# A two-layer hybrid decoder trunk on one core: block inverse on four row strips, score products in bursts of sixteen, low-rank products of both halves in one burst

## The chip, the cores and the metric

One core of a Trainium2 chip runs the whole program. The metric is the device time of one execution in microseconds (us); lower is better. Before the change the median of three runs is 2336.88 us (2336.01 to 2342.26).

## The reference

A residual stream x of 1024 tokens by 1024 channels passes through two layers. Each normalizes it, projects it once to a wide row, gives the parts of that row to three causal token mixers (pooling, retention, RWKV-7), gates and projects the three results, merges them, projects once more and adds. The part that matters here is RWKV-7: 8 heads of 64 channels, with a state that is updated token by token.

```python
def rwkv7_time_mix(p, shift_mu, w0, w2, a0, a2, k_k, k_a, r_k, ln_w, ln_b):
    ...
    w = -jax.nn.softplus(-(w0 + jnp.tanh(wl) @ w2)) - 0.5
    decay = jnp.exp(-jnp.exp(w.astype(jnp.float32)))
    a = jax.nn.sigmoid(a0 + al @ a2)
    ...
    def step(S, inp):
        r_t, w_t, k_t, v_t, a_t, b_t = inp
        sa = jnp.einsum('bhvk,bhk->bhv', S, a_t)
        S = (S * w_t[:, :, None, :] + sa[..., None] * b_t[:, :, None, :]
             + v_t[..., None] * k_t[:, :, None, :])
        return S, jnp.einsum('bhvk,bhk->bhv', S, r_t)
    _, y = lax.scan(step, jnp.zeros((B, H, N, N), jnp.float32), xs)
    ...

def hybrid_layer(x, c_act, positions, ...):
    mod = c_act @ w_ada + b_ada
    shift, scale, gate = jnp.split(mod[:, None, :], 3, axis=-1)
    h = rms_norm(x, norm_g) * (1.0 + scale) + shift
    proj = h @ w_in
    ...
    branches = jnp.stack([o_pool, o_ret, o_rwkv], axis=2)
    y = jnp.einsum('btnw,nwd->btnd', branches, w_branch)
    gates = jax.nn.sigmoid(gate_logits.reshape(B, T, N_BRANCHES, D))
    merged = jnp.sum(gates * y, axis=2)
    return x + gate * (merged @ w_out)
```

## The kernel before

**The wide products.** Channels lie on the 128 partitions, tokens on the free axis in two halves of 512. Each weight tile is split into a high and a low part (wh, wl), each activation too (hhi, hlo, later oG and olo, mhi and mlo), and three products of 128 rows by 128 columns by 512 tokens replace one in full precision. They go to three accumulators `acc` in PSUM. They are the bulk of TensorE's instructions and are called wide products here.

**The mixers.** They are generators ("tasks") in lanes. The loop over the projection's columns issues wide products; after each, `pump` lets every lane whose due time has come issue a step. A task yields a time after which it wants to go on. A pair of RWKV heads (`rwkv_task(l, hp, ...)`, four per layer, one after another in the lane "rwkv") does, for each half h of the sequence:

- the low-rank products (`lora_mm`): three products for the decay (tile lw) and three for the rate a (tile la), each with 64 rows, alternating between the two 64-row halves of the array; ACT takes them through a tanh into sg and aT;
- elementwise work on DVE, ACT and POOL, transposes (vt, bt);
- the score products (tile g): for groups of four chunks of 64 tokens, each with two heads on the two 64-row halves, eight products of 64 rows to two PSUM banks, after which DVE masks them into Z, GQ and KG.

Then for both halves together the inverse of a unit triangular 64 by 64 matrix for each of 16 chunks by 2 heads is formed. The two 32 by 32 diagonal blocks are inverted on DVE (tiles M and tm). The lower left block is the product of three blocks: m1 = (off-diagonal block) x (first inverse), then m2 = (second inverse) x m1. Each is 32 products of 32 by 32 by 32; all of m1 read partitions 0 to 31 (one strip of 32 rows of the array), all of m2 partitions 32 to 63. They are issued in two bursts of 16 for m1 and two for m2, each to one bank of the pool `mx`, each followed by one copy on ACT. At last a chain over the 16 chunks updates the state (tiles cy, ch, xst, S).

Products in plain fp32 (g, m, and all of 128 columns) are run by the chip as two passes, so the profile has two records for each; the products from split tiles have one.

**What sets the order.** The program first records all operations (`Prog.record`), each with the planner's clock at that point as its priority. `slots` gives the tiles their buffers, `needs` finds which operation must follow which, and `weave` is a list scheduler: with a cost for each operation (`cost`) it simulates the five engines and writes the instructions in the order in which they could start, those of lower priority value first among the ready ones. What it writes is what each engine's queue runs, in order. So a change of a cost or of a dependency shifts where the later products of all tasks stand among the wide ones. For a product of 32 rows the cost before was 32 ns for the load and 32 for the product (`o.load, o.occ`), and a change between products of 128, 64 and 32 rows cost nothing.

**PSUM.** Three banks acc, two `mx` (shared by the mixers), two `cy` and one `ch` (both used by rwkv_task alone, after the start).

Of the kernel before, what the change touches and what calls it, by code (L numbers as in the profile page):

```python
# [18 lines left out]
P = 128  # L19
# [188 lines left out]
class Op:  # L208
    __slots__ = ("eng", "what", "args", "kw", "outs", "ins", "prio", "lane", "pred", "succ", "n", "i",
                 "dur", "occ", "load", "twice", "lock", "est", "start", "end", "left", "table", "acc", "arr", "seq", "know", "waits", "part")  # L210
# [50 lines left out]
class Prog:  # L261


    def __init__(self):
        self.ops, self.bufs, self.width, self.pools = [], [], {}, {}
        self.now = lambda: 0.0
        self.lane = [None]
        for e in ENG:
            setattr(self, e, Engine(self, e))
# [41 lines left out]
    def needs(self):  # L311
# [6 lines left out]
        for chain in self.chains.values():  # L318
            old = []
            for b in chain:  # L320
# [21 lines left out]
                old = mine  # L342
        for o in self.ops:
# [3 lines left out]
    def cost(self, o):  # L347
# [6 lines left out]
        if o.eng == "PE":  # L354
# [3 lines left out]
            o.twice = rhs.dtype != F32R and w != "transpose"  # L358
            if rhs.dtype == F32R:
# [3 lines left out]
            else:  # L363
                o.load, o.occ, o.dur = (55, 53, 272) if k == 64 else (32, 32, 191)
# [41 lines left out]
    def weave(self):  # L406
# [13 lines left out]
        landed, table, pe = [0.0] * 8, 0, [0.0, 0.0]  # L420
# [11 lines left out]
        while len(order) < len(ops):  # L432
# [23 lines left out]
            if e == "PE":  # L456
# [3 lines left out]
                m = max(pe[1], max(pe[0], o.est) + ld)  # L460
                if o.twice:
# [19 lines left out]
            for i in o.succ:  # L481
# [4 lines left out]
                elif kind != "a" and e != "PE":  # L486
# [3 lines left out]
                if r == s:  # L490
# [62 lines left out]
def trunk_kernel(ctx, tc, xT, cvec, pos, vecs, consts, w_ada, w_all, pool_w, lora_w, out):  # L553
# [35 lines left out]
    t_cs = slot("cs", 3)  # L589
    mi = lambda s: t_mi(s)[:, 0:HF]  # L590
# [9 lines left out]
    def cyt(s):  # L600
        return ps_c.tile([P, HF], F32, tag="cy", name=nm(s))

# [603 lines left out]
    def rwkv_task(l, hp, kT, rT, vp, lt, lw):  # L1206
# [17 lines left out]
        bvs = []  # L1224
        for h in range(2):
            cr = slice(8 * h, 8 * h + 8)
            yield wait(*lt[h])
            pss = [mx("lw"), cyt("la")]
            lora_mm(pss, lw, hc, lt[h])
            sg = t_ri("sg")  # L1230
            nc.scalar.activation(sg, pss[0], AF.Tanh, bias=vv(l, "w0", hp), scale=0.5)
            yield 400
            aT = t_ri("aT")
            nc.scalar.activation(aT, pss[1], AF.Tanh, bias=vv(l, "a0", hp), scale=0.5)
# [60 lines left out]
            for q in range(2):  # L1295
# [5 lines left out]
                yield 1300  # L1301
            for q in range(2):
                c0 = 8 * h + 4 * q
                yield wait(AR)
                gps = [mx("g"), cyt("g")]
                for j in range(4):
                    for hd in range(2):
                        rows = slice(64 * hd, 64 * hd + 64)
                        mmul(gps[hd][:, j * P : (j + 1) * P], jt(BK, rows, c0 + j), jt(AR, rows, c0 + j))
                lo, hi = slice(0, 64), slice(64, 128)  # L1310
                for hd in range(2):
                    own, other = (lo, hi) if hd == 0 else (hi, lo)
                    g3 = gps[hd].rearrange("p (u n) -> p u n", n=P)
# [824 lines left out]
```

## Time and profile before

| | us |
|---|---|
| timed runs, median (lowest to highest) | 2336.88 (2336.01 to 2342.26) |
| the profiled execution, its own time | 2333.52 |
| its span, first to last instruction | 2331.7 |
| TensorE busy | 2287.5 (98%) |
| VectorE (DVE) busy | 1442.1 (62%) |
| ScalarE (ACT) busy | 855.8 (37%) |
| GpSimd (POOL) busy | 817.4 (35%) |

The mean clock granted to TensorE over the span is 0.996. A row of the timeline has the start, the time to the last end, engine, line, operation, the tile written and those read, rows and columns of the weights, shape, and the number of instructions that were merged into the row. PE is TensorE's products, PEld its weight loads. Nearly all rows carry one line number, since all operations are issued by the planner's loop; they are told apart by their tiles. The profile leaves out numbers in names, so m1 and m2 both stand as m; m<-G,Z is m1 and m<-Z,G is m2.

### The profile page before, as it was taken

The page shows a single profiled execution, that of the slowest core. Times are in us where ns is not written, and L with a number is a line of the kernel's source. Part 1 is how long each engine was busy: PE and PEld are TensorE (multiplying, and loading weights), DVE is VectorE, ACT ScalarE, POOL GpSimd, SP SyncE. Part 2 cuts the span into 40 slices and gives each one's busy share as a digit, 9 for nine tenths or more (in the row PEclk, how much of TensorE's full clock was granted, in tenths as well). Part 3 has the DMA queues.
Part 4 walks back from the last instruction along what each step waited for, and adds up shares of the span by engine and source line. Part 5 has one row for each costly group of instructions (what it writes and reads, how often), then busy time and mean ns, then how long its engine had stood idle before and what let it go on. Part 6 is the DMA issues. An engine that isn't in the chain of part 4 may idle for free. (4 is left out here: it accounts for less than half of the span.)

```text
span 2331.7 us, 33818 instructions
## 1 busy us (share of the span) xinstructions
PE 2287.5 (98%) x12520; PEld 1907.6 (82%) x12520; DVE 1442.1 (62%) x2826; ACT 855.8 (37%) x1706; POOL 817.4 (35%) x714
## 2 busy tenths in 40 slices
PE   5999999999999999999999999999999999999998
PEld 4888888888888888888887888888788888888888
DVE  8776578468568744669546746855864884413544
ACT  5633442433433333223444334234433423311343
POOL 5222233234142333463442233323323333326441
PEclk9999999999999999999999999999999999999999
DMA  8132112112213325767422211211211131545442
GB/s 283 39 110 78 42 46 92 42 41 70 73 55 99 102 61 178 237 194 250 139 82 64 69 41 44 94 34 49 78 61 42 56 118 52 162 126 163 118 145 82
DMA packets 126517, 227.79 MB, mean 98 GB/s; under 512 B 14352, under 2 KB 17680, under 8 KB 126352
## 3 DMA queue, kind: packets, MB, share of 16 engines
q1 hardware_dynamic: 126352, 225.63, 30.9%
q8 instruction: 98, 1.61, 0.3%
q14 instruction: 67, 0.55, 0.1%
HBM read 176.56 MB, written 49.02 MB: 97 GB/s over the span
## 5 line engine op out<-in xcount | busy, mean ns | idle before, releaser
L549 PE MATMUL acc<-hhi,wh 128*128 128x512 f32 x2000 | 806.7, 403 | 0.0
L549 PE MATMUL acc<-hhi,wl 128*128 128x512 f32 x2000 | 806.6, 403 | 0.0
L549 POOL TENSOR_TENSOR wl<-wr,wh 128x512 fp32r<-128x512 f32 x342 | 458.5, 1341 | 991.4 <-ACT wh L549 947.3
L549 PE MATMUL acc<-hlo,wh 128*128 128x512 f32 x2000 | 805.1, 403 | 0.0
L549 ACT CAST wh<-wr 128x512 fp32r<-128x512 f32 x342 | 212.2, 620 | 655.2 <-PE acc L549 441.7
L549 PEld LDWEIGHTS acc<-hlo,wh 128*128 128x128 f32 x2000 | 378.0, 189 | 66.6 <-issue 2.2
L549 PEld LDWEIGHTS acc<-hhi,wl 128*128 128x128 f32 x2000 | 378.1, 189 | 66.5 <-issue 2.2
L549 PEld LDWEIGHTS acc<-hhi,wh 128*128 128x128 f32 x2000 | 378.2, 189 | 65.6 <-issue 1.1
L549 PE MATMUL acc<-oG,wl 128*128 128x512 f32 x384 | 149.9, 390 | 0.0
L549 PE MATMUL acc<-oG,wh 128*128 128x512 f32 x384 | 149.7, 390 | 0.0
L549 PE MATMUL acc<-olo,wh 128*128 128x512 f32 x384 | 149.7, 390 | 0.0
L549 DVE SCALAR_TENSOR_TENSOR S<-ch,pc,SP 64x64 f32<-64x64 f32 x224 | 63.3, 282 | 91.3 <-PE ch L549 85.2
L549 ACT COPY xst<-Z 64x64 f32<-64x64 f32 x256 | 62.4, 244 | 152.7 <-DVE Z L549 149.5
L549 DVE COPY xst<-cy 64x64 f32<-64x64 f32 x256 | 55.4, 216 | 90.7 <-PE cy L549 65.2
L549 DVE TENSOR_TENSOR tm<-VB 64x30 f32<-64x30 f32 (+14 forms) x240 | 105.4, 439 | 7.4
L549 DVE TENSOR_TENSOR VB<-VB,tm 64x30 f32<-64x30 f32 (+14 forms) x240 | 99.4, 414 | 7.5
L549 DVE COPY Z<-ch 64x128 f32<-64x128 f32 x128 | 36.0, 282 | 93.1 <-PE ch L549 92.5
L549 ACT ACTIVATE gsg<-acc 128x512 f32<-128x512 f32 x88 | 52.4, 596 | 91.9 <-PE acc L549 79.6
L549 PEld LDWEIGHTS acc<-olo,wh 128*128 128x128 f32 x384 | 72.1, 188 | 15.0
L549 PEld LDWEIGHTS acc<-oG,wh 128*128 128x128 f32 x384 | 72.1, 188 | 15.0 <-DVE gs L549 0.2
L549 PEld LDWEIGHTS acc<-oG,wl 128*128 128x128 f32 x384 | 72.1, 188 | 15.0
L549 DVE SCALAR_TENSOR_TENSOR gs<-gs,acc 128x512 f32<-128x512 f32 x64 | 43.7, 684 | 46.1 <-PE acc L549 45.0
(270 smaller groups left out, 3693.6 us busy)
## 6 DMA issues: line engine op xcount, KB each, us to landing
wr<-in_w_all SPq DMA_DIRECT2D x364, 256.0 KB, 2.7
gd<-gsg SPq DMA_DIRECT2D x88, 256.0 KB, 2.0
gs<-gd SPq DMA_DIRECT2D x88, 256.0 KB, 2.8
wada<-in_w_ada SPq DMA_DIRECT2D x70, 256.0 KB, 3.3
ol<-od SPq DMA_DIRECT2D x64, 256.0 KB, 3.2
ringG<-in_w_ada SPq DMA_DIRECT2D x26, 256.0 KB, 5.1
x<-in_xT SPq DMA_DIRECT2D x16, 256.0 KB, 5.0
od<-po SPq DMA_DIRECT2D x16, 256.0 KB, 2.2
```

The costliest lines, as they stand in the source:

```text
L549: f(*[put(x) for x in o.args], **{k: put(x) for k, x in o.kw.items()})
```

## The change

Four things are edited.

- **m1 and m2.** The 32 products of each are dealt to four strips (`quad`): strip g works on partitions 32g to 32g+31, on head g // 2 and on eight of the 16 chunks, and writes to a PSUM bank of its own (mx, cy, ch, cy) on the same partitions. Consecutive products go to strips 0, 1, 2, 3. To bring the operands to the strips, two tiles W1 and W2 (`t_mq`, names mn and mt) are filled by copies on ACT and DVE. Each of m1 and m2 is one burst of 32 products.
- **Score products.** Both groups of four chunks of a half are issued as one burst of 16 products to four banks; the masking on DVE follows for both.
- **Low-rank products.** Both halves h are issued at the head of the task as one burst of 12 products to four banks, and the tanh of both halves follow.
- **The planner.** A new list `bursts` makes every product of a burst wait for everything that any of them waits for (kind "x"), so that none starts before all can. The cost of a product of 32 rows becomes 15 and 15 ns, and a change between 128, 64 and 32 rows costs 110 or 200 ns.

```diff
@@ Prog.needs
+        for a, b in self.bursts:
+            own = [o for o in self.ops[a:b] if o.eng == "PE"]
+            union = {q for o in own for q in o.pred if not a <= q < b}
+            for o in own:
+                for q in union:
+                    o.pred.setdefault(q, "x")
@@ Prog.cost
-                o.load, o.occ, o.dur = (55, 53, 272) if k == 64 else (32, 32, 191)
+                o.load, o.occ, o.dur = (55, 53, 272) if k == 64 else (15, 15, 191)
@@ Prog.weave
+                if o.rows != rows:
+                    m, rows = m + (110 if o.rows == 32 else 200), o.rows
@@ rwkv_task
+        yield wait(*lt[0], *lt[1])
+        pss = [[mx("lw"), cyt("la")], [cht("lw"), cyt("la")]]
+        at = len(nc.ops)
+        for h in range(2):
+            lora_mm(pss[h], lw, hc, lt[h])
+        nc.bursts.append((at, len(nc.ops)))
...
-            for q in range(2):
-                c0 = 8 * h + 4 * q
-                yield wait(AR)
-                gps = [mx("g"), cyt("g")]
+            yield wait(AR)
+            gps = [[mx("g"), cyt("g")], [cht("g"), cyt("g")]]
+            at = len(nc.ops)
+            for q in range(2):
                 for j in range(4):
                     for hd in range(2):
-                        rows = slice(64 * hd, 64 * hd + 64)
-                        mmul(gps[hd][:, j * P : (j + 1) * P], jt(BK, rows, c0 + j), jt(AR, rows, c0 + j))
+                        rows, c = slice(64 * hd, 64 * hd + 64), 8 * h + 4 * q + j
+                        mmul(gps[q][hd][:, j * P : (j + 1) * P], jt(BK, rows, c), jt(AR, rows, c))
+            nc.bursts.append((at, len(nc.ops)))
...
+        W1, W2 = t_mq("mn"), t_mq("mt")
+        quad = [(slice(32 * g, 32 * g + 32), g // 2, slice(8 * (g % 2), 8 * (g % 2) + 8)) for g in range(4)]
+        for rows, hd, c8 in quad[1:]:
+            nc.scalar.copy(q4(W1, rows), Z[0:32, c8, 64 * hd + 32 : 64 * hd + 64])
...
-        for q in range(2):
-            ps = mx("m1")
-            for u in range(16):
-                uu = 16 * q + u
-                mmul(ps[32:64, u * 32 : u * 32 + 32], N_[0:32, uu, 32:64], t1(slice(0, 32), uu))
...
+        def quads(name, lhsT, rhs):
+            pss = [mx(name), cyt(name), cht(name), cyt(name)]
+            at = len(nc.ops)
+            for v in range(8):
+                for g, (rows, hd, c8) in enumerate(quad):
+                    u, o = 2 * (c8.start + v) + hd, slice(32 * v, 32 * v + 32)
+                    mmul(pss[g][rows, o], lhsT(g, rows, u, o), rhs(g, rows, u, o))
+            nc.bursts.append((at, len(nc.ops)))
+            return pss
...
+        for g, (rows, hd, c8) in enumerate(quad):
+            (nc.scalar.copy, nc.vector.tensor_copy)[g % 2](W2[rows, 0:256], pss[g][rows, 0:256])
```

TensorE's order at the block inverse of the first pair of heads, before: the two bursts of m1 (m_325 and m_326), three wide products between them, five more, and then m2.

```order
L549 MATMUL m_325_1814<-G_1077,Z_918 32x32 x16
L549 MATMUL acc_1761<-hhi_606,wh_1717 128x512
L549 MATMUL acc_1761<-hlo_618,wh_1717 128x512
L549 MATMUL acc_1761<-hhi_606,wl_1723 128x512
L549 MATMUL m_326_1838<-G_1077,Z_918 32x32 x16
L549 MATMUL acc_1761<-hhi_627,wh_1717 128x512
L549 MATMUL acc_1761<-hlo_641,wh_1717 128x512
L549 MATMUL acc_1761<-hhi_627,wl_1723 128x512
L549 MATMUL acc_1789<-hhi_540,wh_1717 128x512
L549 MATMUL acc_1789<-hlo_556,wh_1717 128x512
L549 MATMUL m_327_1864<-Z_918,G_1077 32x32 x16
```

The same place after: the head of the one burst of m1, whose four banks m_327 to m_330 belong to the four strips (this round of four stands there eight times).

```order
L561 MATMUL acc_1785<-hhi_565,wh_1715 128x512
L561 MATMUL m_327_1838<-G_1116,Z_940 32x32
L561 MATMUL m_328_1840<-mn_1202 32x32
L561 MATMUL m_329_1842<-mn_1202 32x32
L561 MATMUL m_330_1844<-mn_1202 32x32
```

And what stands between its last product and the one burst of m2:

```order
L561 MATMUL m_330_1844<-mn_1202 32x32
L561 MATMUL acc_1785<-hlo_582,wh_1715 128x512
L561 MATMUL acc_1785<-hhi_565,wl_1723 128x512
L561 MATMUL acc_1785<-hhi_616,wh_1715 128x512
L561 MATMUL acc_1785<-hlo_630,wh_1715 128x512
L561 MATMUL acc_1785<-hhi_616,wl_1723 128x512
L561 MATMUL acc_1785<-hhi_638,wh_1715 128x512
L561 MATMUL acc_1785<-hlo_650,wh_1715 128x512
L561 MATMUL m_331_1890<-mt_1835 32x32
```

Four bursts have become two, with seven wide products between them; for the eight blocks of both layers it is seven in six of them, six in one and four in one. Over the program the before has 18 bursts of 16 products and 7 of 32, the after 16 of 32.

TensorE's score products, before, where a burst broke (third pair of heads, first layer): the four products of one half of the array, a wide product, the four of the other half. Elsewhere the two banks alternate in a burst of eight.

```order
L549 MATMUL acc_4524<-hhi_373,wh_4409 128x512
L549 MATMUL g_4572<-AR_4281,BK_4460 128x128 x4
L549 MATMUL acc_4524<-hlo_388,wh_4409 128x512
L549 MATMUL g_4582<-AR_4281,BK_4460 128x128 x4
L549 MATMUL rvt_4588<-cst,rv_4393 128x128 x4
```

After (first pair of heads, the middle of a burst): the second group of four chunks follows the first at once, here from banks g_1080 and g_1083 to g_1094 and g_1096.

```order
L561 MATMUL g_1080<-AR_701,BK_902 128x128
L561 MATMUL g_1083<-AR_701,BK_902 128x128
L561 MATMUL g_1094<-AR_701,BK_902 128x128
L561 MATMUL g_1096<-AR_701,BK_902 128x128
L561 MATMUL g_1094<-AR_701,BK_902 128x128
```

The before has 30 bursts of 8 and 4 of 4; the after 16 of 16, none broken.

TensorE's low-rank products at the first pair of heads, before: one half's six products, and wide ones behind them (the other half's follow 200 rows later).

```order
L549 MATMUL lw_788<-lt_733,lw_527 128x512
L549 MATMUL la_791<-lt_733,lw_527 128x512
L549 MATMUL lw_788<-lt_740,lw_527 128x512
L549 MATMUL la_791<-lt_740,lw_527 128x512
L549 MATMUL lw_788<-lt_733,lw_538 128x512
L549 MATMUL la_791<-lt_733,lw_538 128x512
L549 MATMUL acc_786<-hlo_347,wh_448 128x512
```

After: the other half's six (lw_799, la_801) stand right behind.

```order
L561 MATMUL lw_788<-lt_733,lw_538 128x512
L561 MATMUL la_792<-lt_733,lw_538 128x512
L561 MATMUL lw_799<-lt_737,lw_527 128x512
L561 MATMUL la_801<-lt_737,lw_527 128x512
L561 MATMUL lw_799<-lt_746,lw_527 128x512
L561 MATMUL la_801<-lt_746,lw_527 128x512
L561 MATMUL lw_799<-lt_737,lw_538 128x512
L561 MATMUL la_801<-lt_737,lw_538 128x512
L561 MATMUL acc_786<-hlo_347,wh_448 128x512
```

The before has 17 such bursts (15 of 6, one broken in two), the after 8 of 12. On ACT the order grows from 1697 to 1761 instructions, on DVE from 2826 to 2866; POOL has as many as before, and SP issues four DMAs fewer (86 gate tiles are stored early and fetched again instead of 88).

More of the change, by code (lines that the diff above doesn't have):

```diff
@@ L209 @@
     __slots__ = ("eng", "what", "args", "kw", "outs", "ins", "prio", "lane", "pred", "succ", "n", "i",
-                 "dur", "occ", "load", "twice", "lock", "est", "start", "end", "left", "table", "acc", "arr", "seq", "know", "waits", "part")
+                 "dur", "occ", "load", "twice", "lock", "est", "start", "end", "left", "table", "acc", "arr", "seq", "know", "waits", "part", "rows")
 class Engine:
@@ L267, in __init__ @@
         self.lane = [None]
+        self.bursts = []
         for e in ENG:
@@ L1363, in rwkv_task @@
         )
-        for b in range(2):
+        for i, (rows, hd, c8) in enumerate(quad[1:]):
+            (nc.scalar.copy, nc.vector.tensor_copy)[i % 2](
+                q4(W1, rows, 1), GQ[0:32, c8, 32 * hd : 32 * hd + 32]
+            )
+        for b in (1, 0):
             q = slice(32 * b, 32 * b + 32)
@@ L1380, in rwkv_task @@
-        yield wait(G)
-        for q in range(2):
-            ps = mx("m2")
-            for u in range(16):
-                uu = 16 * q + u
-                mmul(ps[0:32, u * 32 : u * 32 + 32], t1(slice(32, 64), uu), N_[32:64, uu, 32:64])
-                if u % 16 == 15:
-                    yield 600
-            nc.scalar.copy(
-                N_[0:32, 16 * q : 16 * q + 16, 32:64], ps[0:32, :].rearrange("p (u s) -> p u s", s=32)
-            )
-        nc.vector.tensor_copy(GQ[0:64, :, 0:64], Z[0:64, :, 0:64])
@@ new lines, in rwkv_task @@
+        half2 = lambda t, rows, o: t[rows, 256 + o.start : 256 + o.stop]
+        yield 1000
+        yield wait(W1, G)
+        pss = quads(
+            "m1",
+            lambda g, rows, u, o: W1[rows, o] if g else N_[0:32, u, 32:64],
+            lambda g, rows, u, o: half2(W1, rows, o) if g else t1(rows, u),
+        )
+        for g, (rows, hd, c8) in enumerate(quad):
+            (nc.scalar.copy, nc.vector.tensor_copy)[g % 2](W2[rows, 0:256], pss[g][rows, 0:256])
+        nc.scalar.copy(GQ[64:128, :, 0:64], Z[0:64, :, 64:128])
@@ new lines, in rwkv_task @@
+        nc.vector.tensor_copy(GQ[0:64, :, 0:64], Z[0:64, :, 0:64])
+        yield 800
+        yield wait(W2)
+        pss = quads(
+            "m2",
+            lambda g, rows, u, o: W2[rows, o],
+            lambda g, rows, u, o: half2(W2, rows, o) if g != 1 else N_[32:64, u, 32:64],
+        )
+        for g, (rows, hd, c8) in enumerate(quad):
+            (nc.scalar.copy, nc.vector.tensor_copy)[g % 2](
+                GQ[64 * hd : 64 * hd + 32, c8, 32:64], q4(pss[g], rows)
+            )
```

45 lines of the change are left out of this document (24 added, 21 removed).

## The prediction

> **What bounds the kernel now.** I read the page's first part, then the waits of TensorE, then TensorE's busy time by stretches of the span, then the timeline around the bursts that the change touches.
>
> ```profile
> span 2331.7 us, 33818 instructions
> PE 2287.5 (98%) x12520; PEld 1907.6 (82%) x12520; DVE 1442.1 (62%) x2826; ACT 855.8 (37%) x1706; POOL 817.4 (35%) x714
> ```
>
> TensorE is busy 98% of the span; nothing else is above 62% except its own weight loads. The waits of TensorE between 58 us, where the wide projection products set in, and 2031 us, the end of the mixer stage of the second layer (us in total, times, longest; the first two and the last of seven rows, none of which names m, g, lw or la):
>
> ```profile
> PE rot L549 <- DVE yc L549: 5.1, 2, 2.8
> PE cy L549 <- ACT y L549: 1.2, 4, 0.3
> ...
> PE acc L549 <- POOL hlo L549: 0.2, 1, 0.2
> ```
>
> The stretches of that time (width, then busy PE, PEld, DVE, ACT, POOL, granted clock, DMA share, GB/s) show that TensorE does not stop in them:
>
> ```profile
> 58.00:919.50 861.50, 859.96 (x4907) 715.75 (x4908) 567.98 (x1186) 337.54 (x697) 274.04 (x250) 1.00 0.24 74
> 923.00:2028.00 1105.00, 1103.17 (x6000) 915.51 (x6000) 710.14 (x1381) 398.05 (x804) 395.58 (x341) 1.00 0.31 98
> ```
>
> All the work that is changed lies in these two stretches, where 861.50 - 859.96 + 1105.00 - 1103.17 = 3.4 us of 1966.5 are idle. So the time is the sum of TensorE's stream there: a microsecond taken from the stream comes off the end, a microsecond of latency elsewhere is covered by the wide projection products around it. The order shows the same 10764 products on TensorE before and after; what can change is the pace inside the bursts, the number of bursts, and the clock.
>
> **Block inverse, pace and switches.** Timeline of TensorE around one burst of 16 products (32 records, two passes each) and around two that stood together (start, length):
>
> ```profile
> 207.17 0.39 PE L549 MATMUL acc<-hlo,wh 128*128 128x512 f32 x1
> 207.40 0.39 PE L549 MATMUL acc<-hhi,wl 128*128 128x512 f32 x1
> 207.72 1.19 PE L549 MATMUL m<-G,Z 32*32 32x32 f32 x32
> 208.84 0.50 PE L549 MATMUL acc<-hhi,wh 128*128 128x512 f32 x1
> 209.18 0.40 PE L549 MATMUL acc<-hlo,wh 128*128 128x512 f32 x1
> ...
> 405.47 0.39 PE L549 MATMUL acc<-hhi,wh 128*128 128x512 f32 x1
> 405.79 2.21 PE L549 MATMUL m<-G,Z 32*32 32x32 f32 x64
> 407.93 0.50 PE L549 MATMUL acc<-hlo,wh 128*128 128x512 f32 x1
> 408.26 0.40 PE L549 MATMUL acc<-hhi,wl 128*128 128x512 f32 x1
> ```
>
> Wide products follow each other every 0.23 us (207.17 to 207.40). From the last wide start before a burst to the second one after it, less two such steps, a burst of 32 records costs 209.18 - 207.40 - 0.45 = 1.33 us, one of 64 costs 408.26 - 405.47 - 0.45 = 2.34. The difference is 1.01 us for 32 records: 31.6 ns each. What is left, 0.32 us, is the fixed price of leaving and re-entering the wide form: the first record starts 0.09 late, the return 0.12, and the second wide product 0.11.
>
> All of a burst's records before use one strip of 32 rows. How strips share the array is shown by the score products, which use halves of 64 rows:
>
> ```profile
> 118.59 0.40 PE L549 MATMUL acc<-hhi,wl 128*128 128x512 f32 x1
> 118.92 1.16 PE L549 MATMUL g<-AR,BK 64*128 64x128 f32 x16
> 120.01 0.50 PE L549 MATMUL acc<-hhi,wh 128*128 128x512 f32 x1
> 120.35 0.40 PE L549 MATMUL acc<-hlo,wh 128*128 128x512 f32 x1
> ...
> 508.81 1.16 PE L549 MATMUL g<-AR,BK 64*128 64x128 f32 x8
> ```
>
> At 118.92 sixteen records that alternate between two halves take 1.16 us. At 508.81 the order has four products of one half alone (one buffer), eight records, and they take the same 1.16 us. So two halves work side by side at twice the rate of one. In the change each product's two passes still stand next to each other on one strip, then the next strip follows. If a strip's second pass waits for its first, and the next strip's first pass runs beside it, exactly two records run at a time, as in the halves, and four strips do not do better than two: 31.6 / 2 = 16 ns. If all four really run at once it is 31.6 / 4 = 8 ns; if they do not share at all, 31.6. I take 16, the value that the g rows show for the same order of passes, and keep 8 and 31.6 as ends.
>
> By the order, the before has 25 bursts (18 of 16 products, 7 of 32), the after 16 of 32. Before: 18 x 1.33 + 7 x 2.34 = 40.3 us. After: 16 x (0.32 + 64 x 0.016) = 16 x 1.34 = 21.4. Saved: 18.9 us (27.0 at 8 ns; 2.8 at 31.6, from nine switches alone).
>
> **Score products.** One burst of 16 records costs 120.35 - 118.59 - 0.45 = 1.31 us. A record by itself lasts 272 ns (least, median and most in the row of that group):
>
> ```profile
> L549 PE MATMUL g<-AR,BK x512: 272/272/373, 118.9 to 1875.0; 64*128 64x128 f32 x171
> ```
>
> So 0.89 of the 1.16 lies between first and last start: 59 ns a record. Sixteen more in the same burst add 16 x 0.057 = 0.92 (a little under 59, since the first step is the longest). Before there are 34 bursts (30 of 8 products, and four of 4 on one half, which last as long): 34 x 1.31 = 44.5. After, 16 bursts of 16: 16 x (1.31 + 0.92) = 35.7. Saved: 8.8 us. Ends: the fixed part of these switches is at least the 0.32 of the m bursts, 18 x 0.32 = 5.8; at most, with the halves' lone bursts counted fully, 9.2.
>
> **Low-rank products.**
>
> ```profile
> 89.30 0.39 PE L549 MATMUL acc<-hhi,wh 128*128 128x512 f32 x1
> 89.95 0.39 PE L549 MATMUL lw<-lt,lw 64*128 64x512 f32 x1
> 89.96 0.39 PE L549 MATMUL la<-lt,lw 64*128 64x512 f32 x1
> 90.19 0.39 PE L549 MATMUL lw<-lt,lw 64*128 64x512 f32 x1
> 90.51 0.50 PE L549 MATMUL acc<-hlo,wh 128*128 128x512 f32 x1
> 90.85 0.40 PE L549 MATMUL acc<-hhi,wl 128*128 128x512 f32 x1
> ```
>
> A burst of six costs 90.85 - 89.30 - 0.45 = 1.10 us; a pair follows a pair in 0.24. Before: 17 bursts (one was split in two), 18.7 us. After: 8 bursts of 1.10 + 3 x 0.235 = 1.80, 14.4. Saved: 4.3 us (ends 3 and 5: nine switches at 0.32 to 0.5).
>
> Here the two halves of a pair start 0.01 us apart (89.95 and 89.96), and the trace quoted so far has no run of records closer than 31.6 ns on average. The Trainium skill ("TensorE: Matmul & The Clock Gate", in the part on the 56 ns gap) says that matmul starts never come closer than about 25 ns however short they are; the pair does not bear that out for two strips. By its figure the 16 m bursts would be 16 x (0.32 + 1.60) = 30.7 us, an estimate, and their term 9.6 instead of 18.9.
>
> **The clock.** The profiled execution holds one stretch at half clock inside the mixer stage. In these windows the number after the five engines' busy times is the granted clock:
>
> ```profile
> 1522.50:1525.90 3.40, 3.40 (x69) 2.79 (x69) 2.68 (x2) 1.65 (x3) 0.94 (x1) 1.00 0.25 72
> 1526.00:1536.20 10.20, 10.20 (x79) 7.81 (x79) 0.69 (x1) 3.25 (x5) 1.26 (x1) 0.50 0.10 26
> 409.80:413.20 3.40, 3.40 (x71) 2.88 (x70) 0.16 (x1) 2.38 (x5) 1.27 (x1) 1.00 0.28 72
> 508.80:512.20 3.40, 3.40 (x24) 2.87 (x24) 1.53 (x4) 1.83 (x5) 1.31 (x2) 1.00 0.18 63
> ```
>
> And the timeline in the first of them:
>
> ```profile
> 1522.62 1.19 PE L549 MATMUL m<-G,Z 32*32 32x32 f32 x32
> 1524.64 1.19 PE L549 MATMUL m<-G,Z 32*32 32x32 f32 x32
> ```
>
> The half clock follows 3.4 us into which two m bursts fell whole, which left about one microsecond for wide products: the clock was cut although TensorE counted as busy. At 409.80 a burst of 64 records in 3.4 us left room for a little more wide work, and the clock stayed. So small bursts count as little activity, and the cut costs 10.2 x 0.5 = 5.1 us. After the change a site has two bursts of about 1.0 us of records with four to seven wide products between them (0.9 to 1.6 us): 3.4 us can no longer hold both bursts whole, so I expect this loss to go: 5.1 us saved against the profiled execution. Ends: 0 (it happens elsewhere) and -5 more (a second one).
>
> **Added copies and waits.** The change adds 64 instructions on ACT and 40 on DVE, 32 rows by 256 columns, and takes fewer, wider ones away. The nearest row is a copy twice as wide:
>
> ```profile
> L549 ACT COPY G<-m x16: 577/577/579, 208.9 to 1922.7; 32x512 f32<-32x512 f32 x16
> ```
>
> At most 64 x 0.58 = 37 us on ACT and 23 on DVE, spread over 1966 us in which they are idle 63% and 38%: at nothing, covered by the wide products. If that cover is gone, at the head of the second m burst, which now waits for four copies from four banks, TensorE stands with all wide products queued behind it, since its stream is in order. The order gives these copies four to seven wide products, 0.9 to 1.6 us; two copies on each engine need some 0.8 plus hand-over. The list of waits of before has none on an m or g product. The order of the retention products around the merge is shifted too; there rot waited 2.8 us at most. I put 2 us on the loss side for all this (ends 0 and 8, the 5.1 us of rot and as much again with half the bursts 0.2 late).
>
> **Sum.** 18.9 + 8.8 + 4.3 = 32.0 us from the stream, 5.1 from the clock, 2 given back: 35.1. Against the profiled execution's own 2333.5 us (its span of 2331.7 and 1.8 around it) that is 2298.4. The median of the timed runs of before stands 3.4 us above that execution, which I carry over unchanged: **2302 us**, 1.5% faster.
>
> **Rivals.**
> - *Strips do not share* (31.6 ns each): for it, that no row of before shows strips of 32 rows side by side; against it, the g rows. 2302 + 16 = 2318 us. Chance 0.10.
> - *Strips share in part*: something that every record needs in turn sets the pace between the two, 24 ns in the middle of 16 and 31.6. For it: the g records never came closer than 59 ns on average, so no row shows a faster rate of issue; against it the starts 0.01 us apart at 89.95. 16 x (0.32 + 64 x 0.024) = 29.7 us instead of 21.4, so 2310 us. Chance 0.15. The skill's page would put it at 2311.
> - *All four strips at once* (8 ns): 8 us less, 2294. For it: nothing in the g rows tells two from four; against it the order of passes. Chance 0.15.
> - *Bursts come late*: with four banks and all inputs awaited by every burst, each of the 32 m and g bursts stands 1 us: 32 us, 2334, no change. Against it: m and g hardly waited before. Chance 0.06.
> - *The clock turns it slower*: if a joined burst of 2.2 us (g, or m without sharing) beside transposes counts as idle, the clock is cut at many sites. Each cut costs 5.1 us; from eight cuts the 35 us are gone and the change is slower by 7. At all 16 m sites it would be 2302 + 82 = 2384. For it: the cut at 1526. Against it: at 508.8 two g bursts filled most of 3.4 us, and 409.8 a double m burst, both at clock 1.00. Chance 0.04.
> - *The bursts don't form*: excluded by the order, which has every one of the 40 bursts whole.
>
> **How the numbers follow.** The forecast has 0.50; the first three rivals are also faster by over 0.3% (7 us, about what a measurement of this kernel can tell from no change), so faster has 0.90, same 0.06, slower 0.04. The range for 8 in 10 reaches from all four strips at once with another clock cut gone (2294 - 4 = 2290) to strips that do not share with 2 us of stalls more (2320).
>
> **What the profile of after would show.** A burst of 64 m records about 1.2 us long instead of 2.21 (0.7 by four at once, 1.7 with sharing in part, 2.2 without); g bursts of 32 records, 2.1 us long; low-rank bursts of 12, of about 1.6 us; TensorE's busy time lower by some 32 to 37 us with the same 12520 records; no half clock after an m burst; no wait over 1 us at an m2 or g product. Wrong if a new stretch at half clock stands behind g bursts, if rot waits longer than 5 us at the merge, or if m records keep 31 ns.

## The result, and the profile after

The changed kernel takes **2299.32 us** (median of 4 runs, 2295.99 to 2301.11) against 2336.45 (2333.94 to 2342.26) for the kernel before beside it: a ratio of 0.9836 (95% interval 0.9815 to 0.9857), 37 us or 1.6% faster. The forecast was 2302. The profiled execution took 2299.37 us of its own, 34.1 less than the profiled execution of before.

The page's head, after (span, then busy time and share of each engine):

```profile
span 2297.6 us, 33901 instructions
PE 2249.1 (98%) x12520; PEld 1879.9 (82%) x12520; DVE 1470.3 (64%) x2866; ACT 871.7 (38%) x1770; POOL 821.2 (36%) x714
```

TensorE still bounds the kernel. Its busy time fell by 2287.5 - 2249.1 = 38.4 us with the same 12520 records, more than the span did: some of the gain has come back as waiting. The timeline of one burst of the block inverse, the same m1 of which before each half, 32 records, took 1.19 us:

```profile
210.41 0.39 PE L561 MATMUL acc<-hhi,wh 128*128 128x512 f32 x1
210.73 0.21 PE L561 MATMUL m<-G,Z 32*32 32x32 f32 x1
210.73 0.23 PE L561 MATMUL m<-mn 32*32 32x32 f32 x3
210.78 0.19 PE L561 MATMUL m<-G,Z 32*32 32x32 f32 x1
210.79 0.20 PE L561 MATMUL m<-mn 32*32 32x32 f32 x3
...
211.41 0.50 PE L561 MATMUL acc<-hlo,wh 128*128 128x512 f32 x1
211.75 0.39 PE L561 MATMUL acc<-hhi,wl 128*128 128x512 f32 x1
```

m<-G,Z is strip 0, m<-mn the other three. They start in rounds of four (one and three), and the rounds follow each other every 0.03 us, which is the pace of a single strip. The rounds themselves tell how this comes about. The program has the product of strip 0, with its two records, then that of strip 1, and so on; on the chip one record of each strip starts before any strip starts its second. So all four strips run at once: over the 64 records of a burst 0.562 us lie between the first and the last start, 8.9 ns a record. By the same reckoning as in the prediction the burst costs 211.75 - 210.41 - 0.45 = 0.89 us, where 1.34 was forecast.

A low-rank burst of twelve (its first and its last row), and a burst of the score products, now 32 records:

```profile
91.34 0.39 PE L561 MATMUL acc<-hhi,wh 128*128 128x512 f32 x1
91.66 0.49 PE L561 MATMUL lw<-lt,lw 64*128 64x512 f32 x1
...
92.93 0.39 PE L561 MATMUL la<-lt,lw 64*128 64x512 f32 x1
93.25 0.50 PE L561 MATMUL acc<-hlo,wh 128*128 128x512 f32 x1
93.59 0.40 PE L561 MATMUL acc<-hhi,wl 128*128 128x512 f32 x1
...
121.76 0.40 PE L561 MATMUL acc<-hlo,wh 128*128 128x512 f32 x1
122.09 2.06 PE L561 MATMUL g<-AR,BK 64*128 64x128 f32 x32
124.08 0.50 PE L561 MATMUL acc<-hhi,wl 128*128 128x512 f32 x1
124.41 0.39 PE L561 MATMUL acc<-hhi,wh 128*128 128x512 f32 x1
```

They cost 1.80 us (93.59 - 91.34 - 0.45; forecast 1.80) and 2.20 (124.41 - 121.76 - 0.45; forecast 2.23).

The waits of TensorE between 58 and 2031 us (us in total, times, longest) have grown from 8.2 us, the sum of that list before, to 13.0 (the first four and the last of eight rows):

```profile
PE cy L561 <- DVE G L561: 4.3, 3, 2.3
PE rkv L561 <- ACT rkt L561: 2.5, 1, 2.5
PE acc L561 <- DVE mlo L561: 2.0, 2, 1.7
PE m L561 <- DVE mn L561: 1.4, 2, 0.7
...
PE m L561 <- DVE mt L561: 0.4, 2, 0.2
```

The wait of rot for yc, 5.1 us before, is gone. New ones stand in its place, the first at the head of the chain over the chunks (cy), where TensorE waits for a copy of m2's result on DVE. And the half clock is still there, in other places (the number after the engines is the granted clock):

```profile
55.50:62.30 6.80, 6.19 (x15) 4.84 (x16) 6.34 (x11) 6.67 (x10) 5.40 (x5) 0.50 0.24 63
775.70:779.10 3.40, 2.12 (x68) 1.22 (x67) 3.27 (x5) 2.87 (x5) 2.71 (x3) 1.00 0.02 5
779.10:785.90 6.80, 5.70 (x19) 4.96 (x20) 3.33 (x9) 2.72 (x9) 1.91 (x2) 0.50 0.44 155
1526.00:1536.20 10.20, 10.20 (x61) 8.77 (x61) 5.28 (x18) 3.89 (x13) 1.30 (x1) 1.00 0.10 26
```

The stretch at 1526 is at full clock now. But two others of 6.8 us have come, one where the wide work sets in, ahead of every product that the change touches, and one behind the last block inverse of the first layer. Half of 13.6 us is lost after, half of 10.2 + 3.4 (another stretch, at 2031.1) before: 6.8 us in both.

### The profile page after: what moved, and what is told of

It reads as the page before. It is cut to its first block, busy times and chain, and to the rows that moved or that the text cites. A ratio compares the mean times of both kernels' runs of the same rounds, so it can differ in the third digit from the quotient of the medians.

```text
span 2297.6 us, 33901 instructions
## 1 busy us (share of the span) xinstructions
PE 2249.1 (98%) x12520; PEld 1879.9 (82%) x12520; DVE 1470.3 (64%) x2866; ACT 871.7 (38%) x1770; POOL 821.2 (36%) x714
## 5 line engine op out<-in xcount | busy, mean ns | idle before, releaser
L561 DVE TENSOR_TENSOR VB<-VB,tm 64x30 f32<-64x30 f32 (+14 forms) x240 | 107.1, 446 | 7.0
L561 DVE TENSOR_TENSOR tm<-VB 64x30 f32<-64x30 f32 (+14 forms) x240 | 97.6, 407 | 7.1
L561 DVE COPY xst<-cy 64x64 f32<-64x64 f32 x256 | 55.5, 217 | 72.7 <-PE cy L561 45.6
L561 DVE SCALAR_TENSOR_TENSOR mrg<-gs,acc 128x512 f32<-128x512 f32 x32 | 21.9, 686 | 93.0 <-PE acc L561 93.0
```

The costliest lines, as they stand in the source:

```text
L561: f(*[put(x) for x in o.args], **{k: put(x) for k, x in o.kw.items()})
```

## The experiments

All ratios are to the kernel before, timed beside them on the same chip, in three rounds. The changed kernel was not timed again with them; where a run is compared with it, that is by its ratio from the result above and by the two profiles. The theory after the result: the time follows TensorE's stream, the four strips run at once because records of different strips start out of the program's order, and what the bursts save is partly given back to waits and to the clock. The rivals are named where they are tested.

### Only the block inverse changed

The low-rank and score products were issued as before, each group of four chunks and each half by itself; m1 and m2 stay on four strips.

```diff
-        for h in range(2):
-            lora_mm(pss[h], lw, hc, lt[h])
-        nc.bursts.append((at, len(nc.ops)))
...
+            lora_mm(pss, lw, hc, lt[h])
...
+                gps = [mx("g"), cyt("g")]
...
-            nc.bursts.append((at, len(nc.ops)))
```

> The change's block inverse and planner, with the score products and the low-rank products issued as before. Theory (the three terms add, and the block inverse gives 25.9 us because four strips run at once, 0.90 us a burst): g bursts of 16 records at 1.31 us again, m bursts as in the changed kernel, and a time of 2336 - 26 plus up to 5 us of new waits, 2310 to 2316 us. Rival (the forecast's term: two strips at once, 18.9 us, and the rest of the gain is from the joined bursts): 2318 us or more. If the terms don't add because the waits move: under 2306 or over 2320.

Measured: 2306.84 us, ratio 0.9882 (0.9866 to 0.9898). m bursts cost 0.90 us as in the changed kernel. The time was 3 us below the expected range. In this kernel's profile only one half-clock stretch is left, 56.1 to 62.9, so that it lost 3.4 us to the clock instead of 6.8. The block inverse alone brings about three quarters of the gain (0.0118 of 0.0164).

### All on one strip, bursts joined

m1 and m2 stand in one burst of 32 products each as after, but on one strip as before, to two banks, and the copies that the strips need are gone; the planner's cost for such a product is 32 ns again.

```diff
-            for v in range(8):
-                for g, (rows, hd, c8) in enumerate(quad):
-                    u, o = 2 * (c8.start + v) + hd, slice(32 * v, 32 * v + 32)
-                    mmul(pss[g][rows, o], lhsT(g, rows, u, o), rhs(g, rows, u, o))
+        for uu in range(32):
+            o = uu % 16 * 32
+            mmul(pss[uu // 16][32:64, o : o + 32], N_[0:32, uu, 32:64], t1(slice(0, 32), uu))
...
```

> The change with the block inverse left on one strip of 32 rows, its 32 products of m1 and of m2 joined to one burst each (two banks), without the copies to other strips. Theory (the strips carry the term, joining alone nine switches of 0.32): bursts of 64 records at 2.34 us, m costs 16 x 2.34 = 37.4 us, 23 more than in the changed kernel; 2336 - 16.5 = 2320 us, less up to 5 us of waits that the copies cause. Rival (joining is what gains): within 4 us of the changed kernel's 2299.

Measured: 2315.20 us, ratio 0.9917 (0.9899 to 0.9934). Its timeline at the first block:

```profile
209.06 0.39 PE L561 MATMUL acc<-hhi,wl 128*128 128x512 f32 x1
209.38 2.21 PE L561 MATMUL m<-G,Z 32*32 32x32 f32 x64
211.52 0.50 PE L561 MATMUL acc<-hhi,wh 128*128 128x512 f32 x1
211.85 0.40 PE L561 MATMUL acc<-hlo,wh 128*128 128x512 f32 x1
```

64 records on one strip take 2.21 us as in the joined bursts of before, 2.34 with the switches. Against 0.89 that is 16 x 1.45 = 23 us more in the stream. It loses 5.1 us less to the clock (1.7 instead of 6.8), 3.1 less in waits (9.9 instead of 13.0) and has none of the 1.6 us of other gaps that the strips' bursts have: 13.4 net, where the two profiled executions differ by 13.1 (2312.45 and 2299.37). So joining and the strips are separate gains. In the block inverse the strips are by far the larger: 23 us of the stream, where nine switches fewer save 40.3 - 37.4 = 2.9. Over the whole change they come out alike: all joined bursts without the strips bring 0.0083 of the time, the strips 0.0081 more.

### Two strips at a time

For the first half of a burst strips 0 and 1 take turns, then strips 2 and 3.

```diff
-            for v in range(8):
-                for g, (rows, hd, c8) in enumerate(quad):
+            for g0, v in [(g0, v) for g0 in (0, 2) for v in range(8)]:
+                for g, (rows, hd, c8) in list(enumerate(quad))[g0 : g0 + 2]:
```

> The change with the products of a burst dealt in another order: strips 0 and 1 in turn for half of the burst, then strips 2 and 3. Theory (each strip takes one record per 31.6 ns and strips run side by side): two strips at a time make 15.8 ns a record, a burst of 64 costs 0.31 + 1.0 = 1.33 us instead of 0.90, 7 us more in all, 2306 us. Rival (the 8.9 ns a record of the changed kernel are a limit of issue, which two strips reach as well): bursts stay at 0.90 us and the time at 2299.

Measured: 2302.20 us, ratio 0.9861 (0.9846 to 0.9876). The timeline of the first burst (its first record, and the wide products around it):

```profile
208.97 0.39 PE L561 MATMUL acc<-hhi,wh 128*128 128x512 f32 x1
209.29 0.21 PE L561 MATMUL m<-G,Z 32*32 32x32 f32 x1
...
210.34 0.50 PE L561 MATMUL acc<-hlo,wh 128*128 128x512 f32 x1
210.68 0.39 PE L561 MATMUL acc<-hhi,wl 128*128 128x512 f32 x1
```

In the median burst the starts spread over 0.916 us, 14.5 ns a record, and it costs 1.24 us: about the pace of 16 ns that the prediction had taken for all four strips, and the theory here, not the rival. Against 0.89 that is 5.5 us more in 16 bursts; with 1.7 less lost to the clock and 1.8 less in waits (11.2 instead of 13.0), 2.0 net, where the profiled executions differ by 2.0 (2301.32 and 2299.37). The pace is what this run shows; the ratios lie only 0.0025 apart, and their intervals overlap.

### Strip after strip

All eight products of strip 0, then those of strip 1, and so on. The rival here: each strip has a queue of its own, so the order would not matter.

```diff
-            for v in range(8):
-                for g, (rows, hd, c8) in enumerate(quad):
+            for g, (rows, hd, c8) in enumerate(quad):
+                for v in range(8):
```

> The change with the products of a burst dealt strip by strip: eight products (16 records) of strip 0, then eight of strip 1, and so on. Theory (records start in the order of the program except that a few later ones may pass one that waits for its own strip): mostly one strip at a time, 31.6 ns a record, a burst near 2.3 us, 22 us more than the changed kernel, 2321 us. Rival (each strip has a queue of its own, deep enough for the whole burst): all strips still run at once, bursts of 0.9 us, 2299 us. In between if the reach is some records: the pace in the trace tells how many.

Measured: 2314.20 us, ratio 0.991 (0.9892 to 0.9927). Neither number came exactly, but it is far nearer to the theory. The timeline at the hand-over from strip 0 (m<-G,Z) to strip 1:

```profile
211.91 0.59 PE L561 MATMUL m<-G,Z 32*32 32x32 f32 x13
212.32 0.21 PE L561 MATMUL m<-mn 32*32 32x32 f32 x1
212.34 0.19 PE L561 MATMUL m<-G,Z 32*32 32x32 f32 x1
...
212.38 0.19 PE L561 MATMUL m<-G,Z 32*32 32x32 f32 x1
...
212.41 0.19 PE L561 MATMUL m<-G,Z 32*32 32x32 f32 x1
212.43 1.39 PE L561 MATMUL m<-mn 32*32 32x32 f32 x45
```

Strip 1's first record starts when three records of strip 0 are still to come (212.34, 212.38, 212.41; three in each of the eight m1 bursts), and for 0.1 us the two strips run side by side. The burst's starts spread over 1.72 us, 27.2 ns a record. So TensorE does start records ahead of the program's order, but reaches only some three records past those that wait. In the changed kernel three is enough: at strip 3's first record the second records of strips 0, 1 and 2 wait. The Trainium skill ("TensorE: Matmul & The Clock Gate", "Step-by-step: what each phase is for") says that products stay in the program's order and only weight loads are pulled ahead; for records on different strips this trace shows otherwise. In a part that does not speak of strips ("Wait — 56ns, not 53.3ns?") the same page of the Trainium skill says that starts never come closer than about 25 ns; here it is 8.9 on average.

### Score products on four quarters

If four strips run at once, could the score products use more of the array? Each of their products was split by the weights' columns into two of 64 by 64, to four quarters of the array.

```diff
+                if k == 64 and o.ins[0].free_size() == 64:
+                    o.load = o.occ = 15
...
-                    for hd in range(2):
+                    for k, hd in ((0, 0), (0, 1), (1, 0), (1, 1)):
...
-                        mmul(gps[q][hd][:, j * P : (j + 1) * P], jt(BK, rows, c), jt(AR, rows, c))
+                        out = gps[q][hd][64 * k : 64 * k + 64, j * P : (j + 1) * P]
+                        mmul(out, BK[rows, c, k, :], jt(AR, rows, c))
```

> The change with each score product split in two by columns of its weights (64 rows by 64 columns, on four quarters of the array in turn), so a burst has 64 records instead of 32; the planner's cost for them is 15 ns. Theory (a weight load takes as long as it has columns, 112 ns for 128 and 31.6 for 32, and quarters load side by side as strips do): four records per 58 ns, a burst of 16 x 0.058 + 0.41 = 1.34 us instead of 2.20, 13.7 us less, 2286 us. Rival (two quarters on the same rows load one after the other): 29 ns a record, bursts of 2.2 us, 2299 us. If a load takes the same whatever its columns, 56 ns a record: 4.0 us a burst, 2328 us.

Measured: 2292.09 us, ratio 0.9808 (0.9786 to 0.9829). The time is better, but not for the reason expected. The timeline:

```profile
120.75 1.98 PE L563 MATMUL g<-AR,BK 64*64 64x128 f32 x64
122.66 0.50 PE L563 MATMUL acc<-hhi,wl 128*128 128x512 f32 x1
```

Four quarter records take 109 ns where two halves took 112; a burst costs 2.12 instead of 2.20, 1.3 us in all 16. That is the rival's pace. The waits (8.4 instead of 13.0 us) and the clock (3.4 lost instead of 6.8) are lower by more than the rest of the 7 us. Both also differ between kernels that only the planner's costs tell apart, so this run alone does not show that quarters lower them.

### Only the old costs of the planner

```diff
-                o.load, o.occ, o.dur = (55, 53, 272) if k == 64 else (15, 15, 191)
+                o.load, o.occ, o.dur = (55, 53, 272) if k == 64 else (32, 32, 191)
...
-                if o.rows != rows:
-                    m, rows = m + (110 if o.rows == 32 else 200), o.rows
```

> The change with the planner's costs of before (32 and 32 ns for a product of 32 rows, no price for a change between 128, 64 and 32 rows); bursts and strips as in the change. Theory (the costs only shift where things stand; the records and the bursts set the time): bursts at 0.90, 2.20 and 1.79 us as in the changed kernel, the waits of TensorE other than 13 us by up to 5 either way, 2294 to 2305 us. Rival (the costs carry part of the gain): over 2305 us.

Measured: 2298.40 us, ratio 0.9839 (0.982 to 0.9857), the changed kernel's own within the noise. So the new costs as they are bring nothing that can be measured, and the bursts and strips carry the gain.

### Every product of the block inverse issued four times

A burst then has 256 records, with the same output. It asks how many short records it takes until the clock is cut.

```diff
-            for v in range(8):
+            for v in [v for _ in range(4) for v in range(8)]:
```

> The change with every product of the block inverse issued four times (same operands, same place), so an m burst has 256 records instead of 64; the result is the same. Theory (four strips at 8.9 ns a record, and a burst of 2.3 us counts as little activity for the clock, as one strip did before): 16 x 1.7 = 27 us more, and a clock cut of 3.4 us or longer (1.7 us lost or more) at most of the 16 sites, 2299 + 27 + 27 or more, over 2345 us, with half-clock stretches behind m bursts. Rival (four strips at once count as activity): no new half-clock stretch, 2326 us.

Measured: 2375.77 us, ratio 1.0163 (1.0139 to 1.0188). Two things happened at once. At 8.9 ns a burst should cost 0.3 + 256 x 0.0089 = 2.6 us; the bursts took 4.0 to 7.2 from the first to the last start. The first row of TensorE's waits names no releaser ("issue": the profile shows nothing that TensorE waited for):

```profile
PE m L561 <- issue: 39.2, 20, 2.8
```

The records did not slow down: in the first burst 128 of them start within 1.08 us. Then TensorE stops, for 1.5 to 3.0 us at a time, 17 times in the 16 bursts. In each of the 17 stops a transfer of 16 KB on a DMA queue for instructions (q8) lands, and TensorE goes on 1.2 to 1.5 us after it; this kernel has 122 such transfers, the changed one 98. So the supply of instructions is what ran dry. And the clock was cut behind all eight block inverses, for 3.4 to 10.2 us each; behind the first:

```profile
214.60:224.80 10.20, 8.12 (x296) 6.07 (x283) 2.38 (x5) 1.56 (x5) 0.00 (x0) 0.50 0.02 5
```

The time is above the theory's bound, but its sum was not right: a burst grew by 3.5 to 6.3 us, not by 1.7, and more than half of that is stops that the theory did not have. Since TensorE stood still in these bursts, it stays open whether four busy strips by themselves would have kept the clock.

### Column halves for other full-precision products

The retention products rs and rkv, 128 by 128 in fp32, were split into two of 128 by 64 (shown for rs).

```diff
-                mmul(cl(ps, c), lhsT=cl(kT[h], c), rhs=cl(qT[h], c), start=True, stop=True)
+                for k in range(2):
+                    hf = slice(64 * k, 64 * k + 64)
+                    mmul(cl(ps, c)[hf, :], lhsT=cl(kT[h], c)[:, hf], rhs=cl(qT[h], c), start=True, stop=True)
```

> The change with the retention's products rs and rkv (128 rows, 128 columns) each split in two by columns of the weights, 16 records a burst instead of 8, 32 bursts in all. Theory A (column halves of the full rows load side by side, and there is no price for leaving the wide form when only columns are split): a burst of 0.9 us becomes 0.45, 14 us less, 2285 us. Theory B (side by side, but with the switch's 0.3 us): 32 x 0.13 = 4 us less, 2295 us. Theory C (halves on the same rows load one after the other): no gain, 2299 us, or 2309 with the switch. The pace of the records and the starts around a burst tell the three apart.

Measured: 2309.87 us, ratio 0.9888 (0.9865 to 0.9911), 0.0052 or some 12 us above the changed kernel, as theory C with the switch had it. Its timeline at one group of rs:

```profile
317.48 0.39 PE L561 MATMUL acc<-hhi,wh 128*128 128x512 f32 x1
317.80 1.09 PE L561 MATMUL rs<-rq,rk 128*64 128x128 f32 x16
318.82 0.50 PE L561 MATMUL acc<-hlo,wh 128*128 128x512 f32 x1
319.16 0.40 PE L561 MATMUL acc<-hhi,wl 128*128 128x512 f32 x1
```

The burst is no shorter: two halves start 6 to 7 ns apart, every 109 ns, where one whole record starts every 111. And the split form costs more around the burst, as a switch would: from the wide product ahead to the second one behind it is 319.16 - 317.48 = 1.68 us, in the changed kernel 1.35 (316.48 to 317.83, the group of eight being 1.06 long). The 256 added records make 32 such groups: 32 x 0.33 = 10.6 us, and TensorE's busy time is 11.4 us higher (2260.5). The waits are 3.8 us longer too (16.8). Splitting by columns, unlike splitting by rows, gives nothing here.

### Quarters, with the planner told the measured pace

```diff
-                o.load, o.occ, o.dur = (55, 53, 272) if k == 64 else (15, 15, 191)
+                o.load, o.occ, o.dur = (55, 53, 272) if k == 64 else (9, 9, 191)
+                if k == 64 and o.ins[0].free_size() == 64:
+                    o.load = o.occ = 27
```

(together with the edit of the quarters above)

> The score products on four quarters as before, with the planner told the measured paces (27 ns for a record of a quarter, 9 for a record of the block inverse instead of 15). Theory (the run with quarters was 7 us faster mainly because its waits and clock cuts were fewer, 9 us and 3.4 us of half clock's loss against 13 and 7, the records themselves giving 1.3 us; where the waits fall is set by the order): records as there (2.12 us a burst), and a time between 2290 and 2299 us as the waits fall. Rival (quarters give 7 us by themselves): 2292 us again or less.

Measured: 2289.51 us, ratio 0.9791 (0.9776 to 0.9805): faster than the kernel before, with an interval that lies below the changed kernel's. By its number that is the rival, half a microsecond under the theory's range. But the next kernel, timed beside this one, has the same 9 ns and no quarters and takes 2292.55 us; the two intervals overlap, and 3.0 us is all that the quarters can claim. Its waits sum to 8.5 us; the first two:

```profile
PE rot L563 <- DVE yc L563: 3.1, 1, 3.1
PE cy L563 <- DVE G L563: 2.3, 2, 1.7
```

One half-clock stretch is left, 1969.9 to 1976.7.

### The changed kernel, with 9 ns in the planner for an m product

```diff
-                o.load, o.occ, o.dur = (55, 53, 272) if k == 64 else (15, 15, 191)
+                o.load, o.occ, o.dur = (55, 53, 272) if k == 64 else (9, 9, 191)
```

> The change with the planner's cost for a product of 32 rows at 9 and 9 ns, the pace measured, instead of 15. Theory (order only, waits other than 13 us by up to 5): 2294 to 2304 us. Rival (the waits come from the planner taking the m bursts for longer than they are, 1.2 us instead of 0.9): waits fall to the 9 us of before and the time to 2295 us or less.

Measured: 2292.55 us, ratio 0.9799 (0.9782 to 0.9816); the interval just touches the changed kernel's. Waits are 8.9 us instead of 13.0, which the rival had, as it had the time. But the wait at the chain did not go, so it isn't the length of the m bursts in the planner that makes it:

```profile
PE cy L561 <- DVE G L561: 4.1, 2, 2.3
```

### Without the rule that keeps bursts whole

```diff
-        for a, b in self.bursts:
+        for a, b in ():
```

> The change without the rule that every product of a burst waits for all that any of them waits for. By its order the m products stand in 41 bursts (23 of 16, 18 of 8) instead of 16, the low-rank and score products as in the change but for one broken burst. Theory (a burst has a fixed price of 0.31 us, and a burst of products of fewer strips runs slower): 25 switches more, 8 us, and 3 to 5 for bursts on two strips, 2308 to 2314 us. Rival (a burst that waits for all its inputs costs as much in waits as it saves in switches): 2299 us or less.

Measured: 2318.99 us, ratio 0.9915 (0.99 to 0.9929), 5 us above the expected range. The 16 bursts of m became 41: 18 of 16 records at 0.88 us and 23 of 32 at 1.08, together 40.6 us, as much as before the change. The timeline shows what breaks them:

```profile
207.89 0.50 PE L561 MATMUL acc<-hhi,wh 128*128 128x512 f32 x1
208.32 0.69 PE L561 MATMUL m<-mn 32*32 32x32 f32 x16
```

Strips whose copies are ready go first, alone or in pairs, and the last strip follows by itself behind a wide product, its 16 records at the pace of one strip (0.50 us from the first to the last start). The clock adds a little (8.5 us lost instead of 6.8). So without the added waits the strips gain nothing over one strip (0.9915 here, 0.9917 with whole bursts on one strip); the score and low-rank bursts are then nearly all that is left.

## Why the prediction was right, and where it was not

The time came 3 us below the forecast, but the terms did not come as they were set. Against the profiled execution of before, in us saved:

| term | forecast | measured |
|---|---|---|
| block inverse: 40.3 to 16 bursts of 0.90 | 18.9 | 25.9 |
| score products: 44.5 to 16 of 2.195 | 8.8 | 9.4 |
| low-rank products: 18.7 to 8 of 1.79 | 4.3 | 4.4 |
| clock: 6.8 lost before and after | 5.1 | 0 |
| waits of TensorE: 8.2 to 13.0 | -2 | -4.8 |
| gaps in m bursts that the list of waits has not | 0 | -1.6 |
| sum | 35.1 | 33.3 |
| the two profiled executions, 2333.5 to 2299.4 | | 34.1 |

The same account (bursts, gaps, waits and clock from each profile) gives some 24, 20, 32 and 16 us for the first four experiments, in the order above, where 24.1, 21.1, 32.2 and 18.6 lie between the profiled executions. It closes to 1 us in three of them and to 3 us in the fourth, and that much stays unassigned.

**The stream bounds the time**: held. The time follows the bursts' cost, the waits and the clock to within those 1 to 3 us.

**The pace of the strips**: mis-sized. I let a strip's second record hold back what stands behind it, and so had two records at a time and 16 ns. The step that failed is the inference from the score products: two halves can't tell "two at a time" from "as many as there are strips". The rival of all four strips at once, given 0.15, was the mechanism (8.9 ns a record; 14.5 with two strips, 31.6 with one). Strips that share in part, for which the 25 ns of the Trainium skill would have spoken, did not happen.

**The two other bursts**: held, to 0.6 us and 0.1 us. The fixed price of a switch is read from the timeline and can be counted by the burst.

**The clock**: failed. The stretch at 1526 did go, but 5.1 us were not gained, since others came. The one at 779.1 follows a wait. DVE there, after, from the timeline:

```profile
776.28 0.88 DVE L561 COPY mt<-m 32x256 f32<-32x256 f32 x2
777.19 1.63 DVE L561 COPY G<-Z 64x1024 f32<-64x1024 f32 x1
778.85 0.75 DVE L561 SCALAR_TENSOR_TENSOR po<-pps,vec,silu 128x512 f32<-128x512 f32 x1
779.63 0.87 DVE L561 COPY G<-m 32x256 f32<-32x256 f32 x2
```

The last record of m2 started at 777.71 and ended at 777.92. Its two copies on DVE stood behind a copy of 1.63 us and another mixer's operation; the first of them ended at 780.05, and until then TensorE had nothing wide ahead of cy in its queue (row of TensorE in the same window):

```profile
780.20 1.19 PE L561 MATMUL cy<-VB,G 128*128 128x128 f32 x4 [2.28 <-DVE G L561]
```

This first cy does not read what m2 computed: its operands are VB and the part KG of G, and neither holds anything of m2. What it lacks is its PSUM bank. The change lets strips 1 and 3 of m2 write to the two `cy` banks, and the chain can begin only when DVE has copied the first of them out; the second copy, until 780.51, is still running when cy starts. Before, m2 wrote to `mx`, and the first cy waited at none of the eight sites.

So a window of 3.4 us held 2.12 us of work, most of it an m burst, and the clock was halved in the next two. The wait cost 2.3 us and the clock 3.4. The same wait of 2.3 us stands at this place in two more kernels (column halves, and 9 ns for an m product), and in both a half-clock stretch follows, at 776.4 and 778.7. With the old costs one follows at 777.1, behind a wait of 1.65 us of another mixer's product for the copy of m1 on ACT. The stretch at 55.5 has nothing of the change in it; across the kernels that were run it is 0 to 6.8 us long.

**The waits**: too small by 2.8. I priced the head of the second burst of a site and found it covered, and no start inside an m2 burst was held up by more than 0.4 us. Two m1 bursts had longer gaps: at 1503.40 and 1690.75 the first strips had started and the next waited 0.9 us for DVE's copy into mn, so the planner's rule that a burst starts with all its inputs there holds in its own reckoning, not always on the chip. I did not price the way out of m2, and not that its banks are those of the chain. Between its last record and the first cy the trace has 76 other products before, summed over the eight sites (1 at the least), and 25 after (none at the one above): the burst moved closer to what waits for its banks. The Trainium skill ("TensorEngine Tiling (Array Packing)", "PSUM Bottleneck") warns that after a fourfold gain on TensorE the copies out of PSUM may become the limit; the trace agrees in that TensorE waited for such a copy at three sites, 4.3 us in all, though at 779.63 the copy itself took 0.42 us and came late because of the work ahead of it on DVE. That m2 on other banks would remove this wait was not run.

**The offset**: the median of before stood 3.4 us above its profiled execution, and I carried that over. After, the two are equal (2299.32 and 2299.37). The sum for the profiled execution, 2298.4, was off by 1.0; the forecast of the median by 2.7. The strips' surplus of 7.0 and the offset's 3.4 against the clock's 5.1, the waits' 2.8 and the gaps' 1.6: the total is right partly because the misses cancel.

**Signs named beforehand**: m bursts of 0.7 us for four at once (0.75), g bursts of 2.1 us (2.06), no wait over 1 us at an m2 or g product: seen. TensorE's busy time was to go down by 32 to 37 and went down by 38.4, as four strips at once would have it. "No half clock after an m burst" was not: 779.1 is one.

What stays open: what exactly the clock counts as activity (a window with two whole m bursts was cut before, and one with one burst and a wait after), and why the order of the planner puts the waits of each kernel where it does. Kernels that differ only in the planner's costs (the changed one, the old costs, 9 ns) have ratios from 0.9799 to 0.9839, so 0.4% between two kernels here can come from the order, or the session, alone.

## What to carry to other kernels

Products with 32 rows of contraction should alternate over the four strips product by product, in one unbroken burst: records then start every 8.9 ns instead of 31.6, but only if neighbours in the program's order are on different strips and all inputs are there. A burst costs 0.3 us for leaving and re-entering the wide form, so join small ones as well. Then look at what waits for the burst's result and for its PSUM banks: when it is shortened, the copies behind it need wide products of their own to hide in, and a stall there may cost the clock as well.

## What was not expected of the hardware

- TensorE starts records of different strips out of the program's order, some three records ahead, so four strips reach 8.9 ns a record.
- Splitting the weights' columns gives nothing for these fp32 products: a round of four quarters takes 109 ns as a round of two halves takes 112, and split rs and rkv products made the kernel some 12 us slower.
- Bursts of 256 short records run out of instructions: 39.2 us of "issue" in 16 bursts (20 waits), with a 16 KB transfer of instructions landing in each of the 17 long stops. Those of 64 don't show it.
- The half clock came and went at places with the same code: 1.7 to 8.5 us lost per profiled execution in the kernels with each product issued once.
